# Attention scores as three float32r products of split q and k, in place of float32 matmuls

## The chip, the cores and the metric

The kernel runs on one core of one Trainium2 chip. The metric is the device time of one execution in microseconds (us); a smaller number is better. The engines that matter here are PE (TensorE: matmuls, transposes; PEld is its weight loading), DVE (VectorE), ACT (ScalarE) and the DMA queue that SP issues. Each engine works through its own instruction list in order, and waits at an instruction until the semaphores that it names are set.

## What is computed

One layer of a decoder trunk: 512 positions, width 2048. The normalised input h is multiplied by one wide weight matrix; the result is cut into the streams of a convolution branch and of a differential attention branch, both are gated, merged and projected. The part around the change:

```python
p = h @ w_in[l]
cv, cg, cz, q, k, v, az, m_conv, m_attn = jnp.split(p, offsets, axis=-1)
...
s1 = jnp.einsum("bhqd,bhkd->bhqk", a1, k1).astype(jnp.float32) * scale + bias
s2 = jnp.einsum("bhqd,bhkd->bhqk", a2, k2).astype(jnp.float32) * scale + bias
attn = jax.nn.softmax(s1, axis=-1) - lam * jax.nn.softmax(s2, axis=-1)
return jnp.einsum("bhqk,bhke->bhqe", attn.astype(v.dtype), v)
...
o = rms_norm(o, subln_g) * (1.0 - lam_0)
o = o.reshape(B, S, ATTN_WIDTH) * jax.nn.silu(az)
```

There are 8 heads. Each has two softmax maps with a head dimension of 64, so q (and k) of one head fill 128 partitions: map 0 the partitions 0 to 63, map 1 the partitions 64 to 127. Everything is float32.

## The kernel before

The wide gemms are done as three float32r products: an operand is split into a high part `hi`, rounded to float32r by ACT (line 145, or line 150 with a scale), and a rest `lo = x - hi` by DVE (line 146, or 151), and the products hi·hi, hi·lo and lo·hi are summed in PSUM (`mm3`). h is split once and stays; the weights are split as they come, in steps (`wsplit`, tiles `wh_...` and `wl_...`, 3 buffers each): one ACT cast and one DVE subtraction for 24 matmuls of 128x512. A step of the stage k1 that starts at weight row block 12 has the tiles `wh_k1_12` and `wl_k1_12`.

The stages of the attention part are gemms over all of h in the order v0, q0, k0, q1, k1, v1, q2, k2, q3, k3, az0 to az3; stage q1 gives the q of heads 2 and 3 ("pair 1"), v1 the values of heads 4 to 7. A gemm stage writes 2 PSUM banks (`pg_q1_0`, `pg_q1_1`; a v stage 4) out of a pool of 4 that all gemm stages take in turn. A stage can therefore start only when the banks that it takes over have been read: pv_1_0, the first bank of v1, is the one that held pg_q1_0, and pg_az0_0 the one that held pg_q3_0. In the kernel before, ACT reads those banks: `qT` is q times 1/8 (line 597), `kT` a copy of k (line 602), both float32 in SBUF.

The attention of a head (`head`) is laid over the following gemm stages, since a tile scheduler merges the instructions of the program's parts on each engine: heads 0 and 1 run during q1 and k1, heads 2 and 3 during v1, 4 and 5 during q3 and k3, 6 and 7 during az0 and az1. For each block i of 128 queries (n = 128(i+1) keys) PE makes the scores of both maps into two banks `sc` (line 551), DVE adds the bias and takes the maximum (`mx`, line 554), ACT takes the exponential (556), DVE merges the two maps (562), PE transposes (`pt`, 565), ACT copies (`gt`, 567) and PE multiplies with v (`po`, 569). There are only two `sc` banks, so a block's scores wait for the `mx` of the block before. After its four blocks a head ends with ACT squares (`osq`), a chain of small DVE instructions (`oz`, `or_y`, `or_t`: a reciprocal root by Newton steps, lines 117 to 122), `on` on DVE (581), a transpose `pot` on PE (585) and `oT` on ACT (587).

DVE also does the depthwise convolution: 248 "taps" (`cacc`, lines 497 and 500) which are issued 5 per gemm step (`pump`) in a fixed order together with the subtractions of the weight split (`paced`). `temp` is a pool of NTEMP SBUF tiles (128x512) for all that a head needs.

Of the kernel before, what the change touches and what calls it, by code (L numbers as in the profile page):

```python
# [10 lines left out]
F32R = mybir.dt.float32r  # L11
# [5 lines left out]
P = 128  # L17
# [7 lines left out]
HD = 64  # L25
# [4 lines left out]
    0, 1024, 2048, 3072, 4096, 5120, 6144, 7168, 9216)  # L30
V_BADA, V_GPRE, V_N0, V_CB, V_CNG, V_CNB, V_SUB, V_N = 0, 32, 48, 48, 56, 64, 72, 73
NPAGE = 27
NTEMP = 14
NTEMP2 = 12
PUMP = 5
BG = 0
# [15 lines left out]
def hybrid_trunk(ctx: ExitStack, tc: tile.TileContext, x, c, w_ada, b_ada, g_pre, g_post, w_in,  # L52
                 conv_w, conv_b, cn_g, cn_b, w_conv_out, lam_q1, lam_k1, lam_q2, lam_k2,
                 subln_g, w_attn_out, w_o, out):
    nc = tc.nc
# [7 lines left out]
    pr = ctx.enter_context(tc.tile_pool(name="pr", bufs=KT))  # L63
# [6 lines left out]
    def page(name, dt=F32):  # L70
        return pp.tile([P, S], dt, tag="pg", name=name)

    def pair_of(name, dt=F32R):

        return pr.tile([P, 2, S], dt, tag="pr", name=name)
# [34 lines left out]
    def small(n, name):  # L110
        return sp.tile([P, n], F32, tag=f"sm{n}", bufs=1 if n > 16 else 8, name=name)

    def rsqrt(z, n, name):
        y = small(n, f"{name}_y")
        t = small(n, f"{name}_t")
        yi, zi = y.bitcast(I32), z.bitcast(I32)
        nc.vector.tensor_single_scalar(yi, zi, 1, op=ALU.logical_shift_right)
        nc.vector.tensor_scalar(yi, yi, -1.0, 1597463007.0, op0=ALU.mult, op1=ALU.add)
        for _ in range(3):
            nc.vector.tensor_tensor(t, y, y, op=ALU.mult)  # L120
            nc.vector.scalar_tensor_tensor(t, t, -0.5, z, op0=ALU.mult, op1=ALU.mult)
            nc.vector.scalar_tensor_tensor(y, t, 1.5, y, op0=ALU.add, op1=ALU.mult)
        return y
# [13 lines left out]
    def paced(instruction):  # L137

        if PACE:
            tc.stamp_issue_order_token(instruction.ins, "paced")  # L140
        return instruction

    def split(src, hi, lo, scale=None, pace=False):
        if scale is None:
            nc.scalar.copy(hi, src)  # L145
            i = nc.vector.tensor_tensor(lo, src, hi.bitcast(F32), op=ALU.subtract)  # L146
            if pace:
                paced(i)
        else:
            nc.scalar.mul(hi, src, scale)  # L150
            nc.vector.scalar_tensor_tensor(lo, src, scale, hi.bitcast(F32), op0=ALU.mult, op1=ALU.subtract)
# [35 lines left out]
    with tc.tile_pool(name="ps0", bufs=1, space=PSUM) as ps0, tc.tile_pool(name="ap", bufs=1) as ap:  # L187
# [23 lines left out]
        for kt in range(0, KT - 4, 2):  # L211
            g = pair_of(f"xn_{kt}", F32)
# [220 lines left out]
    def spill(key, g):  # L433
        scratch[key] = dram.tile([P, S], F32, name=f"scratch_{key}")
        nc.sync.dma_start(out=scratch[key], in_=g)
# [4 lines left out]
    def temp(name, dt=F32):  # L440
        return mp.tile([P, S], dt, tag="tmp", bufs=NTEMP, name=name)

    def bank(tag, bufs, name):
        return ps1.tile([P, S], F32, tag=tag, bufs=bufs, name=name)
# [74 lines left out]
    def values(half):  # L519
        ps = [bank("g", 4, f"pv_{half}_{t}") for t in range(NT)]  # L520
        for p0 in range(0, KT, 4):
            raw = wraw(w_in[0], p0, 4, C_V + half * 512, 512, f"v_{half}_{p0}")
            for q0 in (p0, p0 + 2):
                whi, wlo = wsplit(raw[:, q0 - p0:q0 - p0 + 2, :], f"v_{half}_{q0}", True)
                pump(rate[0])
                for k in range(2):
                    hh, hl = h[q0 + k]
                    for t in range(NT):
                        ts = slice(t * P, (t + 1) * P)
                        mm3(ps[t], (hh[:, ts], hl[:, ts]), (whi[:, k, :], wlo[:, k, :]),  # L530
                            q0 + k == 0, q0 + k == KT - 1)
        vt[half] = []
        for t in range(NT):
            g = page(f"v_{half}_{t}")
            nc.scalar.copy(g, ps[t])
            vt[half].append(g)

    def head(hd, qT, kT):
        bias = temp(f"bias_{hd}")
        nc.vector.tensor_scalar_mul(bias, dist, 2.0 ** -(hd + 1))  # L540
        sums = small(8, f"sums_{hd}")
        po = bank("o", 1, f"po_{hd}")
        vv = vt[hd // 4]
        es = slice((hd % 4) * P, (hd % 4 + 1) * P)
        for i in range(NT):
            n = (i + 1) * P
            e = []
            for m in range(2):
                pr = slice(m * HD, (m + 1) * HD)
                sc = bank("s", 2, f"sc_{hd}_{i}_{m}")  # L550
                nc.tensor.matmul(sc[:, :n], qT[pr, i * P:(i + 1) * P], kT[pr, :n], start=True, stop=True)
                t = temp(f"t_{hd}_{i}_{m}")
                mx = small(1, f"mx_{hd}_{i}_{m}")
                nc.vector.tensor_tensor_reduce(t[:, :n], sc[:, :n], bias[:, S - n:], scale=-1.0, scalar=3e38,
                                               op0=ALU.add, op1=ALU.min, accum_out=mx)
                nc.scalar.activation(t[:, :n], t[:, :n], AF.Exp, bias=mx, scale=-1.0,
                                     accum_out=sums[:, m * 4 + i:m * 4 + i + 1])
                e.append(t)
            rc = small(1, f"rc_{hd}_{i}")
            nc.vector.reciprocal(rc, sums[:, 4 + i:5 + i])  # L560
            nc.vector.scalar_tensor_tensor(rc, rc, nlam, sums[:, i:i + 1], op0=ALU.mult, op1=ALU.mult)
            nc.vector.scalar_tensor_tensor(e[0][:, :n], e[1][:, :n], rc, e[0][:, :n], op0=ALU.mult, op1=ALU.add)
            pt = bank("t", 1, f"pt_{hd}_{i}")
            for j in range(i + 1):
                nc.tensor.transpose(pt[:, j * P:(j + 1) * P], e[0][:, j * P:(j + 1) * P], ident)
            gt = temp(f"gt_{hd}_{i}")
            nc.scalar.copy(gt[:, :n], pt[:, :n])
            for j in range(i + 1):
                nc.tensor.matmul(po[:, i * P:(i + 1) * P], gt[:, j * P:(j + 1) * P], vv[j][:, es],
                                 start=(j == 0), stop=(j == i))  # L570
        ss = small(4, f"oss_{hd}")
        sq = temp(f"osq_{hd}")
        for i in range(NT):
            nc.scalar.activation(sq[:, i * P:(i + 1) * P], po[:, i * P:(i + 1) * P], AF.Square,
                                 accum_out=ss[:, i:i + 1])
        z = small(4, f"oz_{hd}")
        nc.vector.scalar_tensor_tensor(z, sums[:, :4], EPS, sums[:, :4], op0=ALU.mult, op1=ALU.mult)
        nc.vector.scalar_tensor_tensor(z, ss, 1.0 / P, z, op0=ALU.mult, op1=ALU.add)
        r = rsqrt(z, 4, f"or_{hd}")
        on = temp(f"on_{hd}")  # L580
        nc.vector.tensor_tensor(on.rearrange("p (i e) -> p i e", e=P), po.rearrange("p (i e) -> p i e", e=P),
                                r.unsqueeze(2).to_broadcast([P, NT, P]), op=ALU.mult)
        pt = bank("t", 1, f"pot_{hd}")
        for i in range(NT):
            nc.tensor.transpose(pt[:, i * P:(i + 1) * P], on[:, i * P:(i + 1) * P], ident)
        oT = temp(f"oT_{hd}")
        nc.scalar.activation(oT, pt, AF.Identity, scale=gsub)
        spill(f"o{hd}", oT)

    for pair in range(4):  # L590
        if pair % 2 == 0:
            values(pair // 2)
        pq = gemm2(w_in[0], C_Q + pair * 256, h, KT, f"q{pair}")
        qs, ks = [], []
        for f in range(2):
            g = temp(f"qT_{pair}_{f}")
            nc.scalar.mul(g, pq[f], HD ** -0.5)
            qs.append(g)
        pk = gemm2(w_in[0], C_K + pair * 256, h, KT, f"k{pair}")
        for f in range(2):  # L600
            g = temp(f"kT_{pair}_{f}")
            nc.scalar.copy(g, pk[f])
            ks.append(g)
        for f in range(2):
            head(pair * 2 + f, qs[f], ks[f])

# [36 lines left out]
    for pair in range(4):  # L643
# [9 lines left out]
        for f in range(2):  # L653
            hd = 2 * pair + f
            g = (page if pair == 3 else temp)(f"sz_{hd}")
# [151 lines left out]
    for c0, name in ((C_MA, "ma"), (C_MC, "mc")):  # L807
        for j in range(8):
# [7 lines left out]
            if name == "ma":  # L816
# [4 lines left out]
                hi, lo = temp(f"oh_{j}", F32R), temp(f"ol_{j}", F32R)  # L821
# [43 lines left out]
    for k in range(8):  # L865
        g = pair_of(f"ya_{k}")
        hi, lo = g[:, 0, :], g[:, 1, :]
# [29 lines left out]
    for j in range(8):  # L897
        py = gemm_y(w_attn_out[0], j * 256, ya, f"ya{j}")
        for f in range(2):
# [3 lines left out]
            g = mgp[:, k % 2, :]  # L903
# [7 lines left out]
    for j in range(8):  # L911
        py = gemm_y(w_conv_out[0], j * 256, yc, f"yc{j}")
        for f in range(2):
            k = 2 * j + f
            g = temp(f"ga_{k}")
# [3 lines left out]
            m = pair_of(f"mgs_{k}")  # L919
            hi, lo = m[:, 0, :], m[:, 1, :]  # L920
# [22 lines left out]
    for n in range(4):  # L943
# [3 lines left out]
        for q0 in range(0, KT, 4):  # L947
            raw = wraw(w_o[0], q0, 4, n * 512, 512, f"o_{n}_{q0}")
            for q1 in (0, 2):
                k0 = q0 + q1  # L950
                if n == 3 and k0 >= KT - RES:
                    for k in range(q1, q1 + 2):
                        hi, lo = page(f"woh_{q0 + k}", F32R), temp(f"wol_{q0 + k}", F32R)
# [15 lines left out]
    for t in range(NT):  # L969
# [9 lines left out]
        for a, b in ((0, 2), (2, 3), (3, 4)) if t == NT - 1 else ((0, 4),):  # L979
            for n in range(a, b):  # L980
                g = xr[:, n, :]
# [32 lines left out]
```

## Time and profile before

| | us |
|---|---|
| median of 3 runs | 1435.92 (1434.68 to 1436.1) |
| the profiled execution: its own time | 1436.9 |
| its span in the trace | 1435.1 |
| PE busy in the span | 1397.3 (97%) |
| DVE busy | 1080.9 (75%) |
| ACT busy | 522.1 (36%) |

Busy times of different engines overlap. Matmuls are pipelined, and a record lasts longer than the time after which the next one may start, so the prices of PE below are mostly taken from start to start. The row "PEclk" of the profile's page is the clock granted to PE, in tenths of 2.4 GHz.

### The profile page before, as it was taken

Reading aid. Unit: us, or ns where it says so; the run is one execution under the profiler, and the core shown is the slowest. Engines: PE = TensorE matmul, PEld = TensorE weight load, DVE = VectorE, ACT = ScalarE, POOL = GpSimd, SP = SyncE. Lnnn points to the kernel's source line nnn. Section 1 sums busy time; section 2 is a strip of 40 time slices with the busy share of each in tenths; the row PEclk is TensorE's granted clock in tenths of the full one; section 3 lists DMA queues with packets and bytes.
Section 4 is the critical chain, followed back from the end, with each engine's and each line's share of the span. In section 5 each row is a group of like instructions: output and inputs, shape, how many; then the busy total and the mean of one; then the engine's idle time right before and its main releaser. Section 6 shows DMA issues by size and latency. Waiting matters only on the chain.

```text
span 1435.1 us, 20362 instructions
## 1 busy us (share of the span) xinstructions
PE 1397.3 (97%) x7999; PEld 1189.5 (83%) x7999; DVE 1080.9 (75%) x1750; ACT 522.1 (36%) x839; POOL 1.8 (0%) x8
## 2 busy tenths in 40 slices
PE   5899999999999999999999999999999999999997
PEld 4676787887777867788999999999998888888885
DVE  6997976988888887588988878777767676526645
ACT  3421333223433244444544444444445223222230
POOL 0000000000000000000000000000000000000000
PEclk9999999999999999999999999999999999999999
DMA  9888732331322322234635655543369875236544
GB/s 301 288 280 304 237 123 92 125 121 59 117 67 96 103 67 84 86 111 142 224 128 192 198 170 174 172 140 121 134 233 350 280 243 181 88 107 231 190 147 147
DMA packets 178338, 238.62 MB, mean 166 GB/s; under 512 B 8689, under 2 KB 119618, under 8 KB 177346
## 3 DMA queue, kind: packets, MB, share of 16 engines
q1 hardware_dynamic: 178242, 237.31, 49.9%
q8 instruction: 63, 1.03, 0.3%
q14 instruction: 33, 0.27, 0.1%
HBM read 210.02 MB, written 27.26 MB: 165 GB/s over the span
## 4 chain that ended last, share of the span: by engine, by line
PE 90%; DVE 5%; DMA 2%; ACT 1%; issue 1%; SPq 0%; DVEq 0%; ACTq 0%
PE pw L167 12%; PE pc L167 11%; PE py_ya L167 6%; PE py_yc L167 6%; PE pv L167 6%; PE pg_az L167 5%; PE pg_q L167 5%; PE pg_k L167 5%; PE x_ma L167 5%; PE x_mc L167 4%; PE z_ma L167 3%; PE y_ma L167 3%; PE y_mc L167 3%; PE z_mc L167 3%; PE x_cz L167 2%; PE y_cz L167 2%
## 5 line engine op out<-in xcount | busy, mean ns | idle before, releaser
L500 DVE SCALAR_TENSOR_TENSOR cacc<-u,cw,cacc 128x511 f32<-128x511 f32 (+14 forms) x240 | 164.4, 728 | 0.0
L167 PE MATMUL pc<-hp,wh_c 128*128 128x512 f32 x512 | 159.9, 397 | 3.0 <-DVE part L369 1.2
L167 PE MATMUL pw<-wh_o,mgs 128*128 128x512 f32 x448 | 140.6, 393 | 0.0
L167 PEld LDWEIGHTS pc<-hp,wh_c 128*128 128x128 f32 x512 | 95.6, 190 | 29.0 <-issue 2.7
L167 PE MATMUL pc<-hp,wl_c 128*128 128x512 f32 x256 | 99.0, 396 | 2.1 <-DVE wl_c L146 2.1
L167 PEld LDWEIGHTS pw<-wh_o,mgs 128*128 128x128 f32 x448 | 84.1, 188 | 18.9 <-ACT fsq L932 0.7
L167 PE MATMUL pw<-wl_o,mgs 128*128 128x512 f32 x224 | 87.2, 389 | 0.0
L369 DVE TENSOR_TENSOR part<-pc,part 128x512 f32<-128x512 f32 x96 | 64.7, 687 | 25.3 <-PE pc L167 25.0
L167 PE MATMUL pv<-wh_v,hp 128*128 128x512 f32 x256 | 82.8, 397 | 0.9 <-DVE part L369 0.9
L167 PE MATMUL pg_q<-hp,wh_q 128*128 128x512 f32 x256 | 82.7, 398 | 0.0
L167 PE MATMUL pg_az<-hp,wh_az 128*128 128x512 f32 x256 | 81.5, 395 | 0.0
L167 PE MATMUL pg_k<-hp,wh_k 128*128 128x512 f32 x256 | 80.1, 392 | 0.0
L167 PE MATMUL py_ya<-ya,wh_ya 128*128 128x512 f32 x256 | 78.7, 389 | 0.0
L146 DVE TENSOR_TENSOR wl_o<-wr_o,wh_o 128x1024 fp32r<-128x1024 f32 x28 | 34.2, 1222 | 52.7 <-ACT wh_o L145 52.7
L145 ACT CAST wh_c<-wr_c 128x1024 fp32r<-128x1024 f32 (+1 forms) x36 | 34.2, 955 | 104.0 <-DMA wr_c<-in_w_in_dram 54.9
L889 DVE SCALAR_TENSOR_TENSOR accg<-adag,cact,accg 128x512 f32<-128x512 f32 x60 | 45.1, 751 | 32.2 <-DMA adag<-in_w_ada_dram 31.1
L145 ACT CAST wh_o<-wr_o 128x1024 fp32r<-128x1024 f32 x28 | 29.5, 1052 | 104.5 <-PE pw L167 93.0
L167 PEld LDWEIGHTS pc<-hp,wl_c 128*128 128x128 f32 x256 | 48.5, 190 | 14.1 <-DVE wl_c L146 3.3
L167 PEld LDWEIGHTS pv<-wh_v,hp 128*128 128x128 f32 x256 | 47.8, 188 | 14.3 <-issue 4.5
L167 PEld LDWEIGHTS pg_az<-hp,wh_az 128*128 128x128 f32 x256 | 47.7, 188 | 12.0 <-issue 2.7
L167 PEld LDWEIGHTS pg_q<-hp,wh_q 128*128 128x128 f32 x256 | 47.2, 188 | 12.4 <-issue 2.8
L167 PEld LDWEIGHTS py_ya<-ya,wh_ya 128*128 128x128 f32 x256 | 48.0, 188 | 9.9
(333 smaller groups left out, 3695.0 us busy)
## 6 DMA issues: line engine op xcount, KB each, us to landing
ada<-in_w_ada_dram SPq DMA_DIRECT2D x128, 256.0 KB, 5.4
wr_ma<-in_w_in_dram SPq DMA_DIRECT2D x16, 1024.0 KB
wr_mc<-in_w_in_dram SPq DMA_DIRECT2D x16, 1024.0 KB, 5.2
adag<-in_w_ada_dram SPq DMA_DIRECT2D x32, 512.0 KB, 5.0
wr_o<-in_w_o_dram SPq DMA_DIRECT2D x16, 1024.0 KB, 5.1
wr_c<-in_w_in_dram SPq DMA_DIRECT2D x28, 512.0 KB, 6.1
wr_v<-in_w_in_dram SPq DMA_DIRECT2D x8, 1024.0 KB, 5.1
wr_q<-in_w_in_dram SPq DMA_DIRECT2D x8, 1024.0 KB, 5.0
```

The costliest lines, as they stand in the source:

```text
L145: nc.scalar.copy(hi, src)
L146: i = nc.vector.tensor_tensor(lo, src, hi.bitcast(F32), op=ALU.subtract)
L167: mm = nc.tensor.matmul(ps, a[p], b[q], start=start and i == 0, stop=stop and i == 2, skip_group_check=more)
L369: nc.vector.tensor_tensor(part[i], ps[f], part[i], op=ALU.add)
L500: paced(nc.vector.scalar_tensor_tensor(cvo[t][:, s:], u[t][:, :S - s], wj, cvo[t][:, s:], op0=ALU.mult, op1=ALU.add))
L889: nc.vector.scalar_tensor_tensor(acc, raw[:, k, :], s1, acc, op0=ALU.mult, op1=ALU.add)
```

## The change

Score operands are split as those of the gemms are: for each of the 8 q tiles, in place of `qT`, ACT writes `qh` (line 150) and DVE `ql` (line 151, a read of the same PSUM bank); for each of the 8 k tiles ACT writes `kh` and DVE `kl` (line 146). Each block's scores become three float32r products per map, in the order hi·hi, hi·lo (kl), lo·hi (ql), and the two maps take turns, each on its half of the array's rows. NTEMP rises from 14 to 16.

```diff
-NTEMP = 14
+NTEMP = 16
...
             e = []
-            for m in range(2):
-                pr = slice(m * HD, (m + 1) * HD)
-                sc = bank("s", 2, f"sc_{hd}_{i}_{m}")
-                nc.tensor.matmul(sc[:, :n], qT[pr, i * P:(i + 1) * P], kT[pr, :n], start=True, stop=True)
+            scs = [bank("s", 2, f"sc_{hd}_{i}_{m}") for m in range(2)]
+            for j, (a, b) in enumerate(((0, 0), (0, 1), (1, 0))):
+                for m in range(2):
+                    half = slice(m * HD, (m + 1) * HD)
+                    nc.tensor.matmul(scs[m][:, :n], qT[a][half, i * P:(i + 1) * P], kT[b][half, :n],
+                                     start=j == 0, stop=j == 2)
+            for m, sc in enumerate(scs):
                 t = temp(f"t_{hd}_{i}_{m}")
...
         for f in range(2):
-            g = temp(f"qT_{pair}_{f}")
-            nc.scalar.mul(g, pq[f], HD ** -0.5)
-            qs.append(g)
+            hi, lo = temp(f"qh_{pair}_{f}", F32R), temp(f"ql_{pair}_{f}", F32R)
+            split(pq[f], hi, lo, HD ** -0.5)
+            qs.append((hi, lo))
         pk = gemm2(w_in[0], C_K + pair * 256, h, KT, f"k{pair}")
         for f in range(2):
-            g = temp(f"kT_{pair}_{f}")
-            nc.scalar.copy(g, pk[f])
-            ks.append(g)
+            hi, lo = temp(f"kh_{pair}_{f}", F32R), temp(f"kl_{pair}_{f}", F32R)
+            split(pk[f], hi, lo)
+            ks.append((hi, lo))
```

Because the scheduler merges the parts anew, the change also moves instructions that it does not touch. Lines from 549 on have a number 1 to 3 higher in the changed kernel. Two places are shown.

First, DVE at the end of stage k1, where head 1 ends and stage v1 starts (`on_1` ends head 1's chain, `ql_1` and `kl_1` are the rests of pair 1, `wl_v_1_4` is a later step of v1, `bias_2` and `mx_2` belong to head 2). Before:

```order
L500 SCALAR_TENSOR_TENSOR cacc_4_3562<-u_4_2049,cw_110,cacc_4_3562 128x511
L581 TENSOR_TENSOR on_1_2981<-po_1_2862,or_1_y_2968 128x512 [waits DVE_49]
L500 SCALAR_TENSOR_TENSOR cacc_5_3592<-u_5_2052,cw_110,cacc_5_3592 128x511
L500 SCALAR_TENSOR_TENSOR cacc_4_3562<-u_4_2049,cw_110,cacc_4_3562 128x510 [waits DVE_49]
L500 SCALAR_TENSOR_TENSOR cacc_5_3592<-u_5_2052,cw_110,cacc_5_3592 128x510 [waits DVE_49]
L540 TENSOR_SCALAR bias_2_3276<-dist_79 128x512
L554 ISA t_2_0_0_3282,mx_2_0_0_3283<-sc_2_0_0_3280,bias_2_3276 128x128 [waits DVE_49,PE_49]
```

and now:

```order
L122 SCALAR_TENSOR_TENSOR or_1_y_3008<-or_1_t_3009,or_1_y_3008 128x4 [waits DVE_49]
L584 TENSOR_TENSOR on_1_3021<-po_1_2886,or_1_y_3008 128x512 [waits DVE_49]
L146 TENSOR_TENSOR wl_v_1_4_3705<-wr_v_1_4_3702,wh_v_1_4_3704 128x1024 [waits DMAHW0_49,PE_49,Activation_49]
L500 SCALAR_TENSOR_TENSOR cacc_4_3642<-u_4_2049,cw_110,cacc_4_3642 128x509
L500 SCALAR_TENSOR_TENSOR cacc_5_3672<-u_5_2052,cw_110,cacc_5_3672 128x509
L151 SCALAR_TENSOR_TENSOR ql_1_0_3171<-pg_q1_0_3032,qh_1_0_3170 128x512 [waits Activation_49]
L151 SCALAR_TENSOR_TENSOR ql_1_1_3175<-pg_q1_1_3033,qh_1_1_3174 128x512 [waits Activation_49]
L146 TENSOR_TENSOR kl_1_0_3317<-pg_k1_0_3178,kh_1_0_3316 128x512 [waits Activation_49]
L146 TENSOR_TENSOR kl_1_1_3321<-pg_k1_1_3179,kh_1_1_3320 128x512 [waits Activation_49]
L540 TENSOR_SCALAR bias_2_3324<-dist_79 128x512
L500 SCALAR_TENSOR_TENSOR cacc_4_3642<-u_4_2049,cw_110,cacc_4_3642 128x508 [waits DVE_49]
L557 ISA t_2_0_0_3336,mx_2_0_0_3337<-sc_2_0_0_3328,bias_2_3324 128x128 [waits DVE_49,PE_49]
```

Between `on_1` and the first use of head 2's scores there now stand the subtraction of a weight step (before, it came after them), two taps of another pass over the channels, and the four new instructions. The instructions ahead of this piece, from `wl_v_1_2` to `on_1`, are in order: `wl_v_1_2`, `oz`, then the tap of line 497 and four taps of line 500 with five small instructions between them, then six small instructions in a row; before, the chain of small instructions began one weight step earlier, behind `wl_v_1_0`.

Second, PE at the same place. Before:

```order
L167 MATMUL pg_k1_1_3135<-hp_14_1806,wl_k1_12_3240 128x512
L585 MATMUL pot_1_2983<-ident_72,on_1_2981 128x128 [waits DVE_49,PE_49]
L585 MATMUL pot_1_2983<-ident_72,on_1_2981 128x128 x3
L167 MATMUL pg_k1_0_3134<-hp_15_1811,wh_k1_12_3239 128x512 x2
L167 MATMUL pg_k1_0_3134<-hp_15_1811,wl_k1_12_3240 128x512
L167 MATMUL pg_k1_1_3135<-hp_15_1811,wh_k1_12_3239 128x512 x2
L167 MATMUL pg_k1_1_3135<-hp_15_1811,wl_k1_12_3240 128x512
L167 MATMUL pv_1_0_3542<-wh_v_1_0_3548,hp_0_341 128x512 [waits Activation_49]
```

and now:

```order
L167 MATMUL pg_k1_1_3179<-hp_15_1811,wl_k1_12_3284 128x512
L588 MATMUL pot_1_3023<-ident_72,on_1_3021 128x128 [waits DVE_49,PE_49]
L588 MATMUL pot_1_3023<-ident_72,on_1_3021 128x128 x3
L167 MATMUL pv_1_0_3622<-wh_v_1_0_3628,hp_0_341 128x512 [waits DVE_49]
L167 MATMUL pv_1_0_3622<-wl_v_1_0_3629,hp_0_341 128x512
L167 MATMUL pv_1_0_3622<-wh_v_1_0_3628,hp_0_341 128x512
L552 MATMUL sc_2_0_0_3328<-kh_1_0_3316,qh_1_0_3170 128x128 [waits Activation_49]
L552 MATMUL sc_2_0_1_3329<-kh_1_0_3316,qh_1_0_3170 128x128
L167 MATMUL pv_1_1_3623<-wh_v_1_0_3628,hp_0_341 128x512 [waits DVE_49]
L552 MATMUL sc_2_0_0_3328<-kl_1_0_3317,qh_1_0_3170 128x128 [waits DVE_49]
L552 MATMUL sc_2_0_1_3329<-kl_1_0_3317,qh_1_0_3170 128x128
L552 MATMUL sc_2_0_0_3328<-kh_1_0_3316,ql_1_0_3171 128x128
```

The transposes `pot_1` stand behind the whole of k1 now, the first matmul of v1 waits for DVE (for `ql_1_0`) and no longer for ACT, and the first score block of head 2 is cut in two by a full-array matmul of v1. Ahead of this piece, `po_1` on `gt_1_3` (head 1's last block) is followed by the 24 matmuls of `wh_k1_12` and `wl_k1_12` and then by `pot_1`.

The boundary from k3 to az0 is built alike: `on_5`, `wl_az0_8`, `ql_3_0` follow one another on DVE, with no taps between, `pot_5` stands behind all of k3 (before, 12 matmuls ahead of its end), and the first matmul of az0 waits for `ql_3_0`. On ACT the order at the first boundary is now `wh_v_1_2`, the four `osq_1`, `wh_v_1_4`, `oT_1`, `qh_1_0`, `qh_1_1`, `kh_1_0`, `kh_1_1`; before, `wh_v_1_4` came after the copies of pair 1. The first score block of heads 0, 2, 4 and 6 is cut in two in the way shown. In 17 of the 32 score blocks the map that waits second for its bank is passed, and PE's order is map 0 twice, map 1 twice, map 0, map 1.

## Rows read from the trace of the kernel before

**Rows 1.** The page: busy times, and the chain that ended last by engine

```profile
PE 1397.3 (97%) x7999; PEld 1189.5 (83%) x7999; DVE 1080.9 (75%) x1750; ACT 522.1 (36%) x839; POOL 1.8 (0%) x8
...
PE 90%; DVE 5%; DMA 2%; ACT 1%; issue 1%; SPq 0%; DVEq 0%; ACTq 0%
```

**Rows 2.** Windows q0 with k0, q1, k1: length; busy of PE, PEld, DVE, ACT, POOL; PEclk

```profile
287.30:330.82 43.52, 43.52 (x194) 36.04 (x192) 36.22 (x50) 10.49 (x13) 0.00 (x0) 1.00 0.34 113
330.82:363.56 32.74, 32.25 (x157) 22.73 (x155) 28.54 (x77) 13.88 (x40) 0.00 (x0) 1.00 0.23 75
363.56:392.45 28.89, 28.74 (x139) 21.63 (x138) 25.38 (x62) 11.52 (x31) 0.00 (x0) 1.00 0.29 97
```

**Rows 3.** PE timeline, first two score blocks of head 0: start, us, engine, line, op

```profile
330.82 0.39 PE L167 MATMUL pg_q<-hp,wh_q 128*128 128x512 f32 x1
331.13 0.49 PE L551 MATMUL sc<-kT,qT 64*128 64x128 f32 x4
331.56 0.50 PE L167 MATMUL pg_q<-hp,wh_q 128*128 128x512 f32 x1
331.89 0.39 PE L167 MATMUL pg_q<-hp,wl_q 128*128 128x512 f32 x1
332.12 0.62 PE L167 MATMUL pg_q<-hp,wh_q 128*128 128x512 f32 x2
...
333.82 0.70 PE L551 MATMUL sc<-kT,qT 64*128 64x256 f32 x4
334.45 0.50 PE L167 MATMUL pg_q<-hp,wh_q 128*128 128x512 f32 x1
```

**Rows 4.** Groups by shape, 330 to 600 us: count | busy us, mean ns

```profile
L551 PE MATMUL sc<-kT,qT 64*128 64x512 f32 x32 | 9.5, 641 | 0.0
L562 DVE SCALAR_TENSOR_TENSOR t<-t,rc,t 128x512 f32<-128x512 f32 x8 | 6.0, 750 | 0.2
L581 DVE TENSOR_TENSOR on<-po,or_y 128x512 f32<-128x512 f32 x7 | 4.8, 690 | 0.2
L551 PE MATMUL sc<-kT,qT 64*128 64x128 f32 x32 | 4.4, 322 | 0.0
```

**Rows 5.** Timeline of DVE in k1: taps and small instructions of head 1's chain

```profile
382.12 0.72 DVE L500 SCALAR_TENSOR_TENSOR cacc<-u,cw,cacc 128x483 f32<-128x483 f32 x1
382.75 0.16 DVE L117 TENSOR_SCALAR or_y<-oz 128x4 int32<-128x4 int32 x1
382.82 0.72 DVE L500 SCALAR_TENSOR_TENSOR cacc<-u,cw,cacc 128x483 f32<-128x483 f32 x1
...
386.80 0.15 DVE L121 SCALAR_TENSOR_TENSOR or_t<-or_t,oz 128x4 f32<-128x4 f32 x1
386.99 0.16 DVE L122 SCALAR_TENSOR_TENSOR or_y<-or_t,or_y 128x4 f32<-128x4 f32 x1
```

**Rows 6.** Timeline of all engines where k1 ends and v1 starts

```profile
386.13 1.05 ACT L145 CAST wh_v<-wr_v 128x1024 fp32r<-128x1024 f32 x1 [4.34 <-PE pg_k L167]
387.26 1.23 DVE L146 TENSOR_TENSOR wl_v<-wr_v,wh_v 128x1024 fp32r<-128x1024 f32 x1
389.67 0.68 DVE L581 TENSOR_TENSOR on<-po,or_y 128x512 f32<-128x512 f32 x1
390.50 0.63 PE L585 MATMUL pot<-ident,on 128*128 128x128 f32 x4 [0.15 <-DVE on L581]
391.81 1.08 ACT L597 ACTIVATE qT<-pg_q 128x512 f32<-128x512 f32 x2
392.45 0.19 PEld L167 LDWEIGHTS pv<-wh_v,hp 128*128 128x128 f32 x1 [0.37 <-ACT qT L597]
```

**Rows 7.** PE timeline and window at the lower clock; PE's longest later wait

```profile
136.29 0.28 PE L323 MATMUL pm<-halves,accp 128*128 128x1 f32 x2
138.40:145.20 6.80, 6.80 (x24) 5.93 (x24) 2.93 (x7) 2.57 (x5) 0.00 (x0) 0.50 0.64 219
154.79 0.50 PE L167 MATMUL pc<-hp,wl_c 128*128 128x512 f32 x1 [1.30 <-DVE wl_c L146]
```

## The prediction

> **What bounds the kernel now.** I read the page first: PE is busy 1397.3 us, and the chain that ended last lies 90% on PE and 5% on DVE [rows 1]. So time is gained or lost where PE's own work changes, or where PE has to wait. Then the windows of the stages in which heads 0 and 1 run: in q1 PE is busy 32.25 of 32.74 us, in k1 28.74 of 28.89, while DVE has 4.2 and 3.5 us free there and ACT more than half [rows 2]. PE is the bound in each stage, but DVE is not far behind, and DVE is the engine that gets new work. The third view is the timeline at the end of k1 [rows 6]: `on` on DVE starts at 389.67, `pot` follows on PE at 390.50 while k1's matmuls still go on around it, ACT reads the banks of q1 at 391.81, and v1 starts at 392.45 after 0.37 us of idle time. That place is tuned so closely that a few instructions more ahead of the reader of the bank must show.
>
> **The score matmuls themselves.** The records of a float32 score matmul grow from 322 ns at 128 columns to 641 at 512 [rows 4], 0.83 ns a column, or about 2 cycles at 2.4 GHz. 32 blocks hold 64 matmuls, and there are 128 records: a float32 matmul is two passes. A block of 128 keys takes 0.43 us from its start to the next gemm matmul, one of 256 keys 0.63 (331.13 to 331.56, 333.82 to 334.45) [rows 3]. For 128 more columns it grows by 0.20, not by the 0.43 that four passes one after another would need (4 x 128 x 0.83 ns): the two halves of the array already work at the same time, two passes each. What does not grow is 0.43 - 0.20 = about 0.22 us for loading the first weights and draining. This continues as 0.84 and 1.05 us at 384 and 512 keys (extrapolated).
>
> The trace has no float32r score matmul; the nearest rows are the float32r gemm matmuls, which start 0.23 us apart for 512 columns (331.89 to 332.12) [rows 3], so 0.057 us for 128. Three passes in each half, with halves that still overlap, make 0.22 + 0.17 = 0.39, then 0.56, 0.73, 0.90: a gain of 0.04, 0.07, 0.11 and 0.15 us per block. Eight blocks of each size: -3.0 us. That is the whole gain on PE.
>
> Against it stand the four first blocks that are cut in two by a gemm matmul. Each cut pays the change between full array and half array once more: the fixed 0.22, plus 0.08 on the way in (330.82 to 331.13 is 0.31 in place of 0.23), plus 0.10 on the way out (331.56 to 331.89 is 0.33) [rows 3]. 4 x 0.4 = +1.6. The sum on PE is -1.4 us. Bounds: -3.0 if cuts cost nothing; without any overlap of the halves, six passes in a row add 0.17, 0.34, 0.51, 0.68 to the blocks, 8 x 1.70 = 13.6, so +12.2.
>
> Here one rule of the Trainium skill speaks against the new order. In "TensorE: Matmul & The Clock Gate", Part 3, "What overlaps and what doesn't", matmuls are said to start and end strictly in program order. By it 17 blocks in the order 0 0 1 1 0 1 would need four pass times in place of three; with 0.15 us for a middling pass the sum on PE would be +1.2 and not -1.4. The order of before was 0 0 1 1 too, and by that rule a block would have taken three pass times of its four; the growth of 0.20 per 128 columns is two [rows 3], so the trace does not agree, and I keep -1.4.
>
> **The new work on DVE and ACT.** ACT writes `qh` and `kh` where it wrote `qT` and `kT`: nothing changes in count or size. DVE gets 8 `ql` and 8 `kl` of 512 columns. The nearest rows are 0.75 us for a three-operand instruction of that size and 0.69 for a read of PSUM with two operands [rows 4]: 8 x 0.75 + 8 x 0.69 = 11.5 us in all, spread over eight stages, 1.4 to 1.5 each. Where DVE has 3.5 to 7.3 us free in a stage [rows 2] this is hidden by the gemm matmuls. Two of the four pairs (0 and 2) have it so: their q rest falls into k0 and k2, and `kl_0_0` comes while PE still has full-array work in front of it. I price these at nothing but for the wait below. NTEMP 16 makes up for the two tiles more that a pair holds; I price it at nothing.
>
> For pairs 1 and 3 it is not hidden, since there `ql` stands between two gemm stages: the bank that it reads is the one that the next stage writes. Take E as the end of k1's last matmul and go through DVE's list. The 24 matmuls between `po_1` and `pot_1` last 24 x 0.23 = 5.5 us, so `po_1` ends at E - 5.5. The cast `wh_v_1_2` (1.05 us) runs beside it, and `wl_v_1_2` can go from E - 5.4 to E - 4.2 (1.23) [rows 6]. Then five taps with five small instructions between, 0.70 each (382.12 to 382.82), to E - 0.7; six small ones that wait for each other, 0.19 each (386.80 to 386.99) [rows 5], to E + 0.45; `on` 0.69 [rows 4] to E + 1.15. `pot` follows after 0.15 and takes 0.63 [rows 6], to E + 1.9. Meanwhile DVE does `wl_v_1_4` to E + 2.3 and two taps (0.63 each from start to start) to E + 3.6, while ACT does `oT` and `qh_1_0` (0.54 and some 0.65; the pair of copies took 1.08 [rows 6]) to E + 3.2. `ql_1_0` ends at E + 4.35, and the first matmul of v1 starts at about E + 4.4. This is the earliest. DVE can reach `wl_v_1_2` up to 0.9 late, since two taps, two sums, a first tap and a small instruction (some 3.2 us) stand in its order between the merge of head 1's last block and it; I take E + 4.8. Of that 0.63 is `pot`, which was there before, and 0.37 was waited before [rows 6]. The loss is 3.8 us (3.4 to 4.3).
>
> From k3 to az0 the same walk: three taps, two sums (0.75 with their small instruction) and eight small instructions after the `wl`, 5.1 us in place of 4.65, so `on_5` ends at E + 1.6; `wl_az0_8` to 2.75; `qh_3_0` to 3.6, since `pot_5` stands behind the stage here too; `ql_3_0` to 4.35. The loss is 3.4 us (3.0 to 3.9). Both together: +7.2.
>
> What is late next: behind `ql_1_0` on DVE stand `ql_1_1`, `kl_1_0`, `kl_1_1`, the bias, a tap and the first `mx`, 3.5 us, and the second score block waits for that `mx`; PE has nine gemm matmuls (2.1 us) and the cut first block with its changes (0.4 + 0.4, and 0.3 for the gemm matmul's late weights), 3.2 us, so 0.3 us remain. The first blocks of heads 0, 4 and 6 have similar queues (`wl`, `kl`, bias and a tap ahead of `mx`); 0.3 each, +1.2. So far -1.4 + 7.2 + 1.2 = +7.0.
>
> **The clock.** PE ran at half its clock (PEclk 0.50, the level of 1.2 GHz) from 138.40 to 145.20. Ahead of that, from 136.29, it did one-column matmuls only, 2.1 us of it; a plain wait of 1.30 us at 154.79 left the clock at 1.00 [rows 7]. At k1's end the new wait is 4.8 us with only the 0.63 of `pot` inside, at k3's end about 4.4. These are longer than the stretch that was followed by a fall, so I take it that the clock falls at both. If it falls 2.1 us after PE runs dry and stays low for the same 6.8 us, it reaches E + 8.9; PE works from E + 4.8, so 4.1 us of work go at half speed, a loss of 2.0. If it falls only when the wait is over, 6.8 us go at half speed and 3.4 are lost. I take 2.0, since a slower PE gives DVE time to catch up: +4.0 for two. The Trainium skill ("TensorE: Matmul & The Clock Gate", Part 1, "What's actually happening") says so too: the lower clock is the default, and activity lifts it. The stretch at 138.40 agrees with it, but no row shows a fall after a plain wait.
>
> **The sum.** +7.0 + 4.0 = +11.0. On the profiled execution's 1436.9 this is 1447.9. It lies 1.0 above the median of 1435.92, so I forecast 1447.
>
> **The rivals.** (a) The boundaries wait, but the clock stays: +7.0, 1442.9. For it: waits of 1.30 us have left the clock alone [rows 7]. Against it: these are three times as long. (b) No wait at the boundaries. DVE would have to end `ql_1_0` before E, so to be 4 us earlier than my walk; k1 has 3.5 us of free DVE time [rows 2] and the taps ahead could be done while PE is late elsewhere. Then -3.0 to -1.4 remains, and 1.2 less with the `mx` waits gone: 1433 to 1434.5, the side of faster. It decides at E: each 0.1 us behind it costs 0.1. Against it: 24 matmuls end 5.5 us after `po_1`, and the chain from `oz` to `ql_1_0` alone is 8.5 us long. (c) The halves do not overlap with float32r: +12.2 in place of -1.4, so 13.6 more, 1456 to 1460. Only the float32 blocks speak against it [rows 3], and the same operands would have to be slower in a new form. (d) PE keeps program order: 2.6 more, 1449.5.
>
> **How the numbers follow.** Chances: forecast (a fall at one or both boundaries; 1443 to 1451) 0.50, (a) 0.22, (b) 0.12, (c) 0.09, (d) 0.07. The range leaves out (b) and (c): 1439 to 1453, from (a) with stalls at their lower bounds (-0.8), waits for `mx` at nothing and a gain of 3 on PE, to (d) with falls of 3.4 us. What a measurement of this kernel can tell from no change is 0.2%, 2.9 us. The forecast, (a), (c) and (d) are slower, 0.87 (0.01 of (a) ends within 2.9 us); (b) is split: faster 0.05, if the whole 3.0 on PE comes, otherwise the same, which makes 0.08 with that 0.01.
>
> **What the profile after would show.** The waits of PE at `pot` for `on` (1.1 to 2 us) and at `pv` and `pg_az` for `ql` (2 to 3 us), once each; PEclk 0.5 within 10 us behind either; score blocks of 0.39 to 0.90 us from start to next start, for the halves; DVE busy 11 to 12 us more and q0 to k0 unchanged in length. I am wrong if v1 starts within 1 us of k1's end, or if a score block of 512 keys takes over 1.05 us.

## The result, and the profile after

The changed kernel takes 1447.87 us (median of 4 runs, 1445.82 to 1449.47), the kernel before in the same comparison 1435.3 us (1432.18 to 1436.1). The ratio is 1.0091, 95% interval 1.0071 to 1.0111: 0.9% slower, 12.6 us between the medians. The forecast was 1447, from 1439 to 1453. The profiled runs of the two kernels took 1445.82 and 1436.9 us, so the stages below are read from the fastest of the four runs; all four have a mean granted clock of 0.989 to 0.991, where the profiled run of before has 0.995.

The page of the changed kernel, busy times and the chain that ended last, beside [rows 1]:

```profile
PE 1399.9 (97%) x8063; PEld 1197.0 (83%) x8063; DVE 1091.5 (76%) x1766; ACT 522.4 (36%) x839; POOL 1.8 (0%) x8
...
PE 90%; DVE 5%; DMA 2%; ACT 1%; issue 1%; SPq 0%; DVEq 0%; ACTq 0%
```

DVE does 10.6 us more, PE 2.6, and the chain looks the same. The page doesn't show where 12.6 us went; the windows by stage do. Of the changed kernel, the stages q1, k1, v1, q3, k3 and az (length, then busy us and count of PE, PEld, DVE, ACT and POOL, then PEclk):

```profile
327.32:357.98 30.66, 30.55 (x157) 23.31 (x156) 26.52 (x69) 11.80 (x35) 0.00 (x0) 1.00 0.21 64
357.98:392.10 34.12, 29.98 (x154) 22.87 (x152) 31.66 (x77) 15.29 (x39) 0.00 (x0) 0.98 0.31 110
392.10:457.06 64.96, 64.44 (x308) 48.37 (x309) 53.25 (x134) 25.34 (x69) 0.00 (x0) 0.93 0.19 61
500.58:531.20 30.62, 30.51 (x157) 23.23 (x156) 26.56 (x69) 11.81 (x35) 0.00 (x0) 1.00 0.20 66
531.20:565.40 34.20, 30.17 (x154) 22.86 (x152) 29.58 (x73) 15.01 (x38) 0.00 (x0) 0.99 0.31 106
565.40:674.94 109.54, 108.23 (x501) 84.58 (x502) 79.95 (x184) 45.45 (x102) 0.00 (x0) 0.96 0.26 88
```

The same view of the kernel before, for the front (all ahead of v0), v1, q3, k3 and az (q1 and k1 are in [rows 2]):

```profile
0.00:243.67 243.67, 220.23 (x1141) 171.46 (x1142) 190.85 (x320) 77.60 (x116) 1.83 (x8) 0.99 0.74 239
392.45:454.03 61.58, 61.21 (x294) 45.01 (x293) 53.36 (x134) 27.04 (x72) 0.00 (x0) 1.00 0.23 75
497.55:530.32 32.77, 32.49 (x156) 22.97 (x154) 28.33 (x76) 13.74 (x40) 0.00 (x0) 1.00 0.23 73
530.32:559.48 29.16, 28.91 (x139) 21.80 (x138) 25.54 (x61) 12.56 (x32) 0.00 (x0) 1.00 0.22 72
559.48:664.69 105.21, 104.21 (x486) 80.81 (x484) 78.64 (x181) 46.03 (x103) 0.00 (x0) 1.00 0.31 103
```

q1 and q3 are 2.1 us shorter each, in part since head 0's `pot` and one score block moved into k1 (and head 4's into k3). k1 and k3 are 5.2 and 5.0 longer, and in both PE is idle for 4 us, where it had been busy but for 0.2. v1 and az are 3.4 and 4.3 longer, and PEclk is below 1.00 there. The stages from q1 to az (q2 and k2 are 43.52 both times) come to 333.9 us before and 347.6 after, +13.7. The spans differ by 8.9 only: in the trace of before the front holds the stretch at the lower clock of [rows 7], which the trace after does not have (its front ends at 240.18, 3.5 us earlier, with the same code), and what follows az is 1.4 shorter (769.06 us for 770.41).

The end of k1 in the changed kernel, timeline of all engines, beside [rows 6]:

```profile
387.30 0.39 PE L167 MATMUL pg_k<-hp,wl_k 128*128 128x512 f32 x1
388.30 0.69 DVE L584 TENSOR_TENSOR on<-po,or_y 128x512 f32<-128x512 f32 x1
388.91 1.22 DVE L146 TENSOR_TENSOR wl_v<-wr_v,wh_v 128x1024 fp32r<-128x1024 f32 x1
389.13 0.63 PE L588 MATMUL pot<-ident,on 128*128 128x128 f32 x4 [1.44 <-DVE on L584]
390.04 1.41 DVE L500 SCALAR_TENSOR_TENSOR cacc<-u,cw,cacc 128x509 f32<-128x509 f32 x2
390.45 1.08 ACT L150 ACTIVATE qh<-pg_q 128x512 fp32r<-128x512 f32 x2
391.36 1.28 DVE L151 SCALAR_TENSOR_TENSOR ql<-pg_q,qh 128x512 fp32r<-128x512 f32 x2
392.10 0.80 PE L167 MATMUL pv<-wh_v,hp 128*128 128x512 f32 x1 [2.33 <-DVE ql L151]
...
560.82 0.39 PE L167 MATMUL pg_k<-hp,wl_k 128*128 128x512 f32 x1
562.72 0.63 PE L588 MATMUL pot<-ident,on 128*128 128x128 f32 x4 [1.51 <-DVE on L584]
564.65 1.29 DVE L151 SCALAR_TENSOR_TENSOR ql<-pg_q,qh 128x512 fp32r<-128x512 f32 x2 [0.95 <-ACT qh L150]
565.40 1.22 PE L167 MATMUL pg_az<-hp,wh_az 128*128 128x512 f32 x2 [2.05 <-DVE ql L151]
```

The last matmul of k1 starts at 387.30, so E is 387.53 (0.23 later). PE waits 1.44 for `on`, transposes, and waits 2.33 for `ql`; in between DVE does one weight step and two taps, and ACT `oT` and `qh`. v1 starts at E + 4.57. The last four rows are the other boundary: E is 561.05, az0 starts at E + 4.35. There DVE itself is idle for 0.95 us ahead of `ql`: it waits for ACT's `qh`, which comes behind `pot` and `oT`, while at the first boundary DVE is busy right up to `ql`. In [rows 6] v1 started after 0.37 of idle time.

Windows over the two stretches at the lower clock of the changed kernel:

```profile
390.67:400.91 10.24, 8.81 (x26) 5.88 (x27) 7.40 (x21) 2.69 (x8) 0.00 (x0) 0.50 0.08 27
564.75:574.99 10.24, 9.59 (x31) 6.35 (x33) 5.22 (x19) 3.45 (x12) 0.00 (x0) 0.50 0.07 26
```

The clock falls inside each wait, 3.1 and 3.7 us after E, and stays at 1.2 GHz for 10.24 us, of which PE works 8.81 and 9.59.

The score blocks of 512 and of 128 keys, timeline of PE, beside [rows 3]:

```profile
341.23 0.51 PE L552 MATMUL sc<-kh,qh 64*128 64x512 f32 x2
341.56 0.41 PE L552 MATMUL sc<-kl,qh 64*128 64x512 f32 x2
341.80 0.41 PE L552 MATMUL sc<-kh,ql 64*128 64x512 f32 x2
342.14 0.74 PE L167 MATMUL pg_q<-hp,wh_q 128*128 128x512 f32 x2
...
345.96 0.33 PE L552 MATMUL sc<-kh,qh 64*128 64x128 f32 x2
...
346.44 0.50 PE L167 MATMUL pg_q<-hp,wl_q 128*128 128x512 f32 x1
```

A block of 512 keys takes 0.91 us from its start to the next gemm matmul, where six passes one after another, at the 0.23 of a gemm matmul, would take at least 1.38; the halves overlap. One of 128 keys takes 0.48.

### The profile page after: what moved, and what is told of

Read it like the earlier page. It is cut to its first block, busy times and chain, and to the rows that moved or that the text cites. A ratio compares the mean times of both kernels' runs of the same rounds, so it can differ in the third digit from the quotient of the medians.

```text
span 1444.0 us, 20503 instructions
## 1 busy us (share of the span) xinstructions
PE 1399.9 (97%) x8063; PEld 1197.0 (83%) x8063; DVE 1091.5 (76%) x1766; ACT 522.4 (36%) x839; POOL 1.8 (0%) x8
## 4 chain that ended last, share of the span: by engine, by line
PE 90%; DVE 5%; DMA 2%; ACT 1%; issue 1%; SPq 0%; DVEq 0%; ACTq 0%
PE pw L167 12%; PE pc L167 10%; PE pv L167 6%; PE py_ya L167 6%; PE py_yc L167 6%; PE pg_az L167 6%; PE pg_q L167 5%; PE pg_k L167 5%; PE x_ma L167 5%; PE x_mc L167 5%; PE y_mc L167 3%; PE z_mc L167 3%; PE z_ma L167 3%; PE y_ma L167 3%; PE x_cz L167 2%; PE y_cz L167 2%
## 5 line engine op out<-in xcount | busy, mean ns | idle before, releaser
L167 PE MATMUL pg_az<-hp,wh_az 128*128 128x512 f32 x256 | 84.6, 406 | 2.1 <-DVE ql L151 2.1
L167 PEld LDWEIGHTS pg_k<-hp,wh_k 128*128 128x128 f32 x256 | 47.5, 188 | 10.4 <-issue 0.7
```

Source lines behind the costliest of these rows:

```text
L167: mm = nc.tensor.matmul(ps, a[p], b[q], start=start and i == 0, stop=stop and i == 2, skip_group_check=more)
```

## The experiments

Theory A: the time was lost in two waits for DVE at the ends of k1 and k3, and in the lower clock behind them. Theory B: the float32r products in half-array form cost it. Theory C: the new DVE work of some 11 us cost it, wherever it stands. "Sum" below is the length of the stages from q1 to az in the profiled run, 333.9 before and 347.6 after.

**e1: no rests.** q and k as high parts only, in all three products, so part of q and k is left out; NTEMP is 16 as in the changed kernel.

```diff
-            split(pq[f], hi, lo, HD ** -0.5)
-            qs.append((hi, lo))
+            nc.scalar.mul(hi, pq[f], HD ** -0.5)
+            qs.append((hi, hi))
```

> Leaves out the rests of q and k: three float32r products of the high parts alone, so no ql and kl on DVE, the banks read by ACT only, and the output is that of rounded q and k. Theory A (the time was lost in two waits for ql at the ends of k1 and k3, and in the lower clock behind them; the score products themselves gain 1 to 3 us): 1432 to 1435 us, no stretch at the lower clock between 300 and 650 us, v1 starting within 0.5 us of k1's end. Theory B (the float32r products in half-array form, with their changes of form, cost the time): about 1448 us as in the changed kernel.

Measured: 1433.22 us, ratio 0.9987 (0.9976 to 0.9998); sum 332.3, 1.6 less than before; no lower clock between 300 and 650 us. Theory B falls, and so does NTEMP as a cause: the same 192 products, in 16 buffers and without the rests, lose nothing. No block is cut here; blocks that are cut are in e4.

**e2: rests only.** The kernel before with 16 rests that nothing reads.

```diff
             nc.scalar.mul(g, pq[f], HD ** -0.5)
+            lo = temp(f"ql_{pair}_{f}", F32R)
+            nc.vector.scalar_tensor_tensor(lo, pq[f], HD ** -0.5, g, op0=ALU.mult, op1=ALU.subtract)
```

> The kernel before with its float32 scores and NTEMP 16, plus 16 rests ql and kl on DVE that read the gemm banks and that nothing uses. Theory A: both waits and both stretches at the lower clock come back, 1447 to 1451 us (the changed kernel without its gain on the products). Theory B: 1436 us, since DVE has time to spare.

Measured: 1444.62 us, ratio 1.006 (1.0045 to 1.0075). PE's waits from 320 to 640 us (us in total, times, longest):

```profile
PE pot L585 <- DVE on L581: 3.9, 5, 1.5
PE pv L167 <- DVE ql L599: 2.3, 1, 2.3
PE pg_az L167 <- DVE ql L599: 2.0, 1, 2.0
```

The waits at the two boundaries (1.5 us as the longest for `pot`, then 2.3 and 2.0) are within 0.1 us of the changed kernel's, without one float32r score product. The median is 2.4 us below the expected range. In the profiled run the lower clock lasted 6.83 and 3.41 us at the boundaries in place of 10.24 twice, which goes the same way.

**e3: PE kept at work.** The changed kernel with extra matmuls in the two waits.

```diff
+        if pair % 2:
+            dummy = bank("s", 2, f"dummy_{pair}")
+            for r in range(16):
+                nc.tensor.matmul(dummy, h[r % KT][0][:, :P], h[r % KT][0], start=True, stop=True)
         for f in range(2):
             head(pair * 2 + f, qs[f], ks[f])
```

> The changed kernel with 16 extra gemm-sized matmuls into a free score bank at each of the two boundaries, so that PE works while it waits for DVE (3.6 us of work in about 4 us of waiting). Theory A: the waits for ql last as long as before but the clock stays at full, which gives back the 4.4 to 4.8 us of each stretch less up to 1 us: 1439 to 1441 us. If the lower clock costs nothing because DVE is the bound behind the boundary: 1447 to 1449 us.

Measured: 1440.96 us, ratio 1.0037 (1.0024 to 1.005). Timeline of PE at the end of k1:

```profile
388.01 1.98 PE L610 MATMUL dummy<-hp 128*128 128x512 f32 x8
389.83 0.60 PE L588 MATMUL pot<-ident,on 128*128 128x128 f32 x4
390.19 2.08 PE L610 MATMUL dummy<-hp 128*128 128x512 f32 x8
392.53 0.50 PE L167 MATMUL pv<-wh_v,hp 128*128 128x512 f32 x1 [0.26 <-DVE ql L151]
```

Windows of the same kernel over k1, v1 and az:

```profile
358.46:392.53 34.07, 33.47 (x169) 25.84 (x167) 31.62 (x77) 15.06 (x38) 0.00 (x0) 1.00 0.32 107
392.53:453.67 61.14, 60.61 (x309) 45.91 (x309) 53.07 (x134) 25.57 (x70) 0.00 (x0) 1.00 0.21 67
562.10:668.31 106.21, 104.51 (x501) 81.94 (x501) 79.71 (x184) 45.42 (x102) 0.00 (x0) 1.00 0.27 90
```

k1 is as long as in the changed kernel (34.07 against 34.12): v1 starts as late. But the clock stays, and v1 and az are 3.8 and 3.3 us shorter than there. This separates the two terms: the sum is 340.5, so the waits with all else make +6.7 and the clock +7.1. One of the seven runs took 1445.87 us at a mean granted clock of 0.991, so it spent longer at the lower clock, where is not shown; the other six have 0.995 to 0.998.

**e4: own buffers for q and k.** The same instructions, with 8 of the 16 buffers set apart.

```diff
-NTEMP = 16
+NTEMP = 8
...
+    def keep(name, dt=F32):
+        return mp.tile([P, S], dt, tag="qk", bufs=8, name=name)
...
-            hi, lo = temp(f"qh_{pair}_{f}", F32R), temp(f"ql_{pair}_{f}", F32R)
+            hi, lo = keep(f"qh_{pair}_{f}", F32R), keep(f"ql_{pair}_{f}", F32R)
```

> The changed kernel with the same instructions, but qh, ql, kh and kl in 8 SBUF buffers of their own and 8 in the pool for the rest, in place of 16 in one pool. In the order this puts ql_1 and ql_3 into the middle of k1 and k3, and pot_1 and pot_5 ahead of the stages' ends. Theory A: no wait at the boundaries, no lower clock, 1431 to 1434 us, so 2 to 4 us faster than before. Theory C (the 11.5 us of new DVE work is what costs, wherever it stands): 1445 us or more. Theory B: about 1448 us.

Measured: 1434.35 us, ratio 0.9993 (0.9982 to 1.0004): level with before, not clearly faster, and 0.35 us above the expected range; sum 333.4. Timeline of DVE and PE around k1:

```profile
361.92 0.69 DVE L151 SCALAR_TENSOR_TENSOR ql<-pg_q,qh 128x512 fp32r<-128x512 f32 x1 [0.36 <-ACT qh L150]
363.51 0.69 DVE L151 SCALAR_TENSOR_TENSOR ql<-pg_q,qh 128x512 fp32r<-128x512 f32 x1 [0.22 <-ACT qh L150]
...
388.72 0.63 PE L591 MATMUL pot<-ident,on 128*128 128x128 f32 x4
390.12 0.39 PE L167 MATMUL pg_k<-hp,wl_k 128*128 128x512 f32 x1
390.34 0.40 PE L167 MATMUL pv<-wh_v,hp 128*128 128x512 f32 x1
```

`ql` is made as soon as q1 has ended (361.76), and v1 follows k1 without a gap. DVE has the same 16 rests as in the changed kernel, so theory C falls, and the first blocks of four heads are cut in two here as well, so theory B stays out. What differs is the buffers and, with them, where the instructions stand. Of the gain on the products little is left: PE waits 1.2 us for the merged map (`pt` for `t`) between 320 and 640 us, where before it waited 0.4, and 0.5 us for `mx`.

**e5: the product with kl first**, on top of e4, so that no block is cut in two.

```diff
-            for j, (a, b) in enumerate(((0, 0), (0, 1), (1, 0))):
+            for j, (a, b) in enumerate(((0, 1), (0, 0), (1, 0))):
```

> As e4, but the product with kl stands first in every block, so that no block starts before kl is there; in the order none of the 32 blocks is cut by a gemm matmul any more. If a cut costs the 0.4 us that the prediction gave it: 1.6 us less than e4, 1432 to 1433.5 us and 2 to 3.5 us below before. If cuts are nearly free, or the wait for kl takes their place: as e4, 1434 to 1435 us.

Measured: 1435.1 us, ratio 0.9991 (0.9983 to 1.0); sum 333.5. The second branch: all eight blocks of 128 keys take 0.48 now, but nothing is gained over e4. The first block now starts only when `kl` is there, 1.0 us into q1 (0.3 in e4); so `mx` comes later, and the second block waits for it: PE waits 1.9 us for `mx` (four times), 0.5 in e4.

**e6: map by map**, on top of e5.

```diff
-            for j, (a, b) in enumerate(((0, 1), (0, 0), (1, 0))):
-                for m in range(2):
+            for m in range(2):
+                for j, (a, b) in enumerate(((0, 1), (0, 0), (1, 0))):
```

> As e5, but the three products of map 0 stand ahead of the three of map 1 in all 32 blocks (in e5: 11 blocks alternate, 16 in the order 0 0 1 1 0 1, 5 map by map). If each half of the array runs its own matmuls ahead of the other's (the prediction): the same as e5, a block of 512 keys 0.90 us. If matmuls start strictly in program order: five pass times per block in place of 3.8 on average, 5 us more than e5, a block of 512 keys about 1.35 us.

Measured: 1434.22 us, ratio 0.9991 (0.9982 to 1.0); sum 333.5, as in e5. A block of 512 keys:

```profile
341.28 0.51 PE L555 MATMUL sc<-kl,qh 64*128 64x512 f32 x2
341.62 0.41 PE L555 MATMUL sc<-kh,qh 64*128 64x512 f32 x2
341.85 0.41 PE L555 MATMUL sc<-kh,ql 64*128 64x512 f32 x2
342.19 0.50 PE L167 MATMUL pg_q<-hp,wl_q 128*128 128x512 f32 x1
```

The program has map 0 three times and then map 1 three times, the trace shows them two by two, in 0.91 us. The order of the maps in the program did not matter here. So what the beginning says of the engines, that each works through its list in order, does not hold for PE's matmuls on different halves.

**e7: half the fill.** As e3 with 8 and 6 extra matmuls, all ahead of `pot` (`range(8 if pair == 1 else 6)`).

> The changed kernel with only 8 (after k1) and 6 (after k3) of the extra matmuls of e3, all ahead of pot, so that the wait of some 2.2 us behind pot stays empty and the wait ahead of it is filled. If a wait of that length alone lowers the clock: both stretches come back, 1446 to 1449 us. If the clock fell because of both waits together: it stays at 1.00, 1440 to 1442 us as e3. I think the second, since waits of 1.3 us left it alone and nearly half of the gap is filled: 0.6.

Measured: 1444.15 us, ratio 1.0061 (1.0048 to 1.0074). Timeline of PE at the end of k1:

```profile
391.35 0.60 PE L588 MATMUL pot<-ident,on 128*128 128x128 f32 x4
394.09 0.50 PE L167 MATMUL pv<-wh_v,hp 128*128 128x512 f32 x1 [2.13 <-DVE ql L151]
```

Windows over its two stretches at the lower clock:

```profile
395.95:399.36 3.41, 3.41 (x15) 2.21 (x13) 3.25 (x11) 0.88 (x4) 0.00 (x0) 0.50 0.02 5
566.62:573.45 6.83, 6.83 (x26) 4.89 (x27) 2.94 (x16) 2.13 (x9) 0.00 (x0) 0.50 0.00 0
```

I was wrong: the second wait alone, 2.13 us, was followed by the lower clock, though for less time than in the changed kernel, and the result lies between the two expected ranges. v1 and az are 1.5 and 2.3 us longer here than in e3, for stretches of 3.41 and 6.83 us.

**e8: e5 with the splits at the highest priority** (`with tc.high_priority():` around both).

> As e5, with the splits of q and k given the scheduler's highest priority; in the order the first matmul of v1 then waits for nothing, since both banks were read before. What is left to gain over e5 is the wait of at most 0.4 us at each boundary: 0 to 0.8 us less than e5, not more than the measurement can tell.

Measured: 1434.46 us, ratio 0.9994 (0.9985 to 1.0003); sum 333.3. No measurable difference, as expected.

**e9: ACT sets the banks free.** The changed kernel with a float32 copy of q and k in SBUF, from which the split is made.

```diff
-            split(pq[f], hi, lo, HD ** -0.5)
+            full = temp(f"qf_{pair}_{f}")
+            nc.scalar.mul(full, pq[f], HD ** -0.5)
+            split(full, hi, lo)
```

> The changed kernel, but ACT first copies q and k from PSUM to float32 SBUF tiles, and both parts of the split are made from these, so that ACT alone sets the gemm banks free as before; pool and products as in the changed kernel. In the order pot_1 and pot_5 still stand behind all of their stage, and the copy behind oT. If the bank that DVE reads late were the whole cause: no wait for pv and pg_az, 1436 to 1438 us. If the cause is that head 1's and head 5's ends and the splits are placed late, whichever engine reads the bank: pot is awaited as long (1.5 us), pv and pg_az about 1 us less than in the changed kernel, the clock still falls: 1444 to 1447 us. I expect the second.

Measured: 1443.79 us, ratio 1.0052 (1.0033 to 1.0071). PE's waits from 325 to 640 us:

```profile
PE pot L588 <- DVE on L584: 4.6, 7, 1.5
PE pv L167 <- ACT qf L601: 1.3, 1, 1.3
PE pg_az L167 <- ACT qf L601: 1.3, 1, 1.3
```

The second case, 0.2 us below its range: `pot` is awaited as long, the bank 1.0 and 0.8 us less, the clock falls for 3.41 us at both. That DVE reads the bank is a quarter of the waits; the rest is that the ends of heads 1 and 5 and the reads of the banks stand so late. There is also a new wait of 1.6 us, in two pieces, for the rest of a weight step (`wl_az`) in az. One of the four runs took 1439.07 us at a mean granted clock of 0.997, the others 1442.55 to 1446.11 at 0.992 and 0.993: by that, the clock can hardly have fallen at the boundaries in it.

**e10: the kernel before with own buffers** (4 for `qT` and `kT`, 10 for the rest; the edit is as in e4).

> The kernel before with qT and kT in 4 buffers of their own and 10 in the pool for the rest. In the order the copies of pairs 1 and 3 move from the boundary into the middle of k1 and k3. If the pool alone is what makes e4 as fast as before, this gains the same: the 0.37 us waits at the boundaries, 0 to 0.8 us, so 1434.5 to 1436 us, and e4 to e8 hold nothing of the products' own gain of 2 to 3 us.

Measured: 1438.46 us, ratio 1.0019 (1.0011 to 1.0028); sum 336.9. I was wrong here: with 10 buffers for a head, PE waits for the merged map (`pt` for `t`, 2.2 us from 320 to 680 us, in 7 waits; 0.4 in the kernel before). So the own buffers cost about 3 us in the float32 kernel, of which that wait explains 1.8. By the two ratios e4, which has own buffers too (8 for a head and not 10), is 0.26% faster than e10; that e4 to e8 pay the same price for them is not shown, the wait for the merged map being 1.2 us in e4.

## Why the prediction was right, point by point

The mechanism held in each step; one of its sizes, that of the clock, was far off.

- **Where the banks are read (+7.2).** The walk through DVE's list put the end of `on` at E + 1.15 to 2.05 and at E + 1.6, and the starts of v1 and az0 at E + 4.8 (4.4 at the earliest) and E + 4.4. The trace has `on` ending at E + 1.46 and E + 1.52 and the stages starting at E + 4.57 and E + 4.35. Less `pot` and what was waited before, that is 3.6 + 3.4 = 7.0. DVE's new work was priced a little high: the 16 rests took 0.68 to 0.69 each, and DVE was busy for 10.6 us more, not 11 to 12. e2 shows that the rests alone bring the waits, e4 that the same rests in another place do not.
- **The products on PE (-1.4).** Blocks were to take 0.39, 0.56, 0.73 and 0.90 us; they take 0.48, 0.55, 0.72 and 0.90 where nothing else is waited for. Only the smallest was off: it is 0.06 dearer than the float32 block (0.42) and not 0.03 cheaper; its six weight loads may be why, which no run shows. The uncut gain is so 2.5 and not 3.0 us; e1, which has no cuts, shows 1.6 of it in the sum, with 1.1 us of waits for `mx`. A cut block with the gemm matmul inside it takes 1.05 us (327.64 to 328.69 for head 0, the same for head 4), where a whole one and a gemm matmul take 0.48 + 0.23: 0.34 for a cut, where 0.4 was forecast. Together that is -2.5 + 1.4 = -1.1. The overlap of the halves, which rival (c) denied, is there, and e6 rejects rival (d): with all blocks map by map, a block would take five pass times by it, and three were measured. The rule of the Trainium skill that was weighed there ("TensorE: Matmul & The Clock Gate", Part 3, "What overlaps and what doesn't": matmuls start and end in program order) differs from this measurement for matmuls on different halves of the rows, and the measurement decides.
- **The waits for `mx` (+1.2).** They are there, and a little smaller. The second score block of heads 0 and 4 takes 0.76 us in place of 0.55 and starts 0.41 behind the matmul ahead of it in place of 0.32, so it loses 0.3, as priced. Behind the boundaries those blocks ran at half clock, and the wait can't be told apart; in e3, at the full clock, head 6's block loses 0.4 and head 2's nothing, 1.0 for the four. What e3's +6.7 leaves, less 7.0 and plus 1.1 for the products, is 0.8.
- **The clock (+4.0).** It fell at both boundaries, as forecast, against rival (a), but this is the term that was mis-sized: +7.1 by e3, just above the 3.4 for each boundary that the prediction had as its other case. The prediction took the length of the one stretch in the trace of before, 6.8 us, and started it 2.1 us behind E. It lasted 10.24 us, and nearly all of it lay behind the wait (8.81 and 9.59 us of PE's work, so 4.4 and 4.8 us at half speed, of which 3.8 and 3.3 remain in the stages' lengths).
- **The sum.** +11.0 was forecast on top of the profiled execution; the stages have +13.7, and the measured terms, 7.0 - 1.1 + 1.0 + 7.1, come to 14.0. The medians are 12.6 apart. That the forecast of 1447 lies 0.9 us from the measured median is in part luck: by the stages the clock term was 3.1 us short, and the front, which the change does not touch, alone differs by 3.5 us between the two traces.

Rival (b), no wait at the boundaries, is what e4 makes of the change. The prediction gave it 0.12 for the kernel as it was written, since it needed `ql` 4 us earlier; in e4 it starts 0.2 us after q1's end (361.92), in the changed kernel 33 us after it (391.36, where q1 ended at 357.98).

Why the scheduler puts the splits of pairs 1 and 3 so late is argued, not shown. With one pool, the reads of q1's banks come at the end of k1, behind `on` of head 1 (the kernel before at 391.81, the changed one at 390.45, e1 at 390.23, e2 at 395.24, e9 at 394.52), and with a pool of their own they come where q1 ends and k1 starts (e4 at 361.28, e10 at 363.84). So the pool seems to hand out its buffers in the order of the program; that a smaller pool for the rest of the head does it is not ruled out.

## What to carry to other kernels

When a split needs a second read of an accumulator, look first at which stage takes over that bank, and at what stands in front of the reader in its engine's order; with some 11 us of new DVE work the kernel stayed level with before in e4, and lost 13.7 us in the stages where a few of these instructions stood in the wrong place. A PE wait of a few microseconds can be paid twice, as it was at both boundaries here (+7.0 and +7.1), once as a wait and again as a stretch at half clock behind it: price both. Before blaming an operation, try the same instructions with buffers of their own.

## What the runs showed of the hardware

- The lower clock (1.2 GHz) followed plain waits: one of 2.13 us in e7, and one of 2.18 us in the front of e2, after which it came at 41.27; at the same place of the program e4 waited 1.57 us and kept its clock. It lasted 3.41, 6.83 or 10.24 us, and what sets which of them is open: e2 has 6.83 and 3.41 behind waits that in the changed kernel were followed by 10.24 twice. The size of that term is therefore known for these runs only.
- The front, whose lines no edit here touches, has such a stretch of 6.8 us near 140 us in the profile of before, of 3.41 in e1 and e4, and none in the changed kernel's and e3's. The front is 240.18 us long in the changed kernel's trace, 243.67 in that of before and 245.38 in e2's, so changes of 1 to 2 us are hard to tell here.
- The two halves of PE's array run their own matmuls ahead of each other's: three products of one half and then three of the other, 512 columns each, take 0.91 us (e6), as when they alternate.
